# The start of a two-layer decoder trunk: GpSimd loads more of it, and its first turn stands in another order

## The chip, the cores and the metric

The kernel runs on one core of a Trainium2 chip. The metric is the device time of one execution in microseconds. Of the kernel before, three runs give a median of 1202.78 us (1201.39 to 1202.89). One more execution was recorded by the hardware profiler; all rows below come from it.

The names of the engines: PE is TensorE's matmul (PEld its weight load), DVE is VectorE, ACT is ScalarE, POOL is GpSimd, SP is SyncE, which here only issues DMAs. SP and POOL each have a DMA queue of their own (q1 and q0 in the profile), and both use the same 16 DMA engines.

## The reference

Two layers over one sequence of 512 tokens with 1024 channels, all in float32. The change lies in the first layer's first half, which is

```python
shift, scale, gate = adaln_params(c, ada_w[0, 0], ada_b[0, 0])   # silu(c) @ w + b, cut in three
hn = modulate(h, norm_g[0, 0], shift, scale)                     # rmsnorm(h, g) * (1 + scale) + shift
...
u = h @ w_in                                                     # s5_mixer: 64 groups of 16 channels
...
bu_re = jnp.einsum('blgc,gpc->blgp', u_c, bb_re)                 # each group drives 64 complex states
...
y = jnp.einsum('blgp,gcp->blgc', hs_re, cr) - jnp.einsum('blgp,gcp->blgc', hs_im, ci)
```

with a complex diagonal scan over time between the last two, then a gelu, a gated linear unit, an output product and the residual. What follows (a gated ConvFFN, an attention layer, a second ConvFFN, a final norm) is not touched.

## The kernel before

Channels lie on the 128 partitions, in eight tiles (`KT`), and time on the free axis. The start (L1189 to L1260) stands in a block whose order is written by hand for PE, ACT, DVE and SP (`manual_schedule`), the loop over the eight tiles of the state-space layer (from L1315) in a second block of that kind, which also fixes POOL. In each block an engine keeps the order of the code; a scheduler sets how the rows of both blocks follow each other on an engine.

The start, in the order of the code:

- SP loads `first` (c, the state-space parameters), x as `h` (4 transfers), `rest`, then the adaLN weights `raw<-in_ada_w`, 512 KB each. They go into three rings of buffers (`raw`, 3; `w_hi`, 5; `w_lo`, 5), so a load waits until PE has read what lay in its buffer.
- ACT squares x tile by tile, PE sums the squares over the partitions with a matrix of ones (L1197, eight products), ACT copies the sums (L1199), PE turns them (L1202).
- DVE works out the parameters of the state space from `first` (`s5_params`, small instructions of 32 to 256 columns): powers of the complex decay (`s5_pr`, `s5_pi`), the input factors (`s5_lr`, `s5_li`), the magnitude `s5_mag8`; within them the inverse root of the mean square (L427 to L437). POOL works out the turn angles (`s5_turns`).
- `ada_pe(i, (1,))` is *scale*: four steps of two weights each, four column groups of PE at a time (L226), ACT copies the result (`ada_rows`, L235), PE adds the bias and turns it (L165, L170), and DVE makes `ga` of it. DVE then forms `a_x` = h times ga times the inverse root, eight instructions (L1212).
- `ada_pe(i, (0,))` is *shift*, in the same way; between its steps PE takes the products of the first output tile, `first_tile` (L1223), which need only `a_x` and the first input matrix. Since shift is a constant along time, its part of the first tile is a column, `col` (L1245), that ACT adds on evacuation (`uf`, L1259). For the other tiles ACT adds shift to `a_x` (`shift_x`, L1252).
- B (`s5_b`) and C (`s5_rr`) are loaded by SP behind shift's weights; ACT copies B with its signs (`s5_signs_b`, L833 and L834) and flips C's (`s5_signs_c`, L839).

Then a turn for each tile m: `project` (L1270) multiplies a tile of `w_in` into u; `s5_states_in` and `s5_states_out` make tables of 1024 columns on DVE (L994, L1004); `s5_inputs` (L1032) combines them on PE, ACT evacuates them to the matrices `w1` and `kt` (L1037, L1041); `s5_kernel` stores `kt` to a table `s_z` in memory (L1050), `s5_toeplitz` reads it back shifted as `tw` (L1057), and ACT masks it (L1066). u goes to memory and back in another layout (L1276, L1280). `s5_blocks` (L1090) puts u into the states, DVE scans (L1106 to L1121), PE takes the outputs from inputs (L1131) and states (L1142), ACT applies the gelu (`yg`, L1155). Between these stand the steps of `ada` and `ada2`, which make the gate of this half and the scale and shift of the next one with the same L226.

POOL loads what the turns need. What holds it back are small additions called `gate` (L1317, L1343, L1372): each reads two numbers of a tile, so POOL's later instructions wait until that tile is there. Before, the first gate reads `mag8`, the second `tw` of turn 0, the third `tw` of turn 1. Some 23 loads of adaLN weights pass behind them.

## Time and profile before

| | |
|---|---|
| three runs, median (lowest, highest) | 1202.78 us (1201.39, 1202.89) |
| the profiled execution | 1208.49 us |
| its span, first to last instruction | 1206.7 us |
| busy: PE, PE's weight loads, DVE, ACT, POOL | 1178.1, 1019.4, 1009.1, 614.8, 122.9 us |
| granted PE clock, mean over the span | 0.994 |
| moved by DMA | 182.00 MB, of it 137.94 on SP's queue, 41.95 on POOL's |

Each row of an order of time gives start and duration in us, engine, line, operation, output and input tiles, shapes and count; rows of one kind that follow each other are merged, and brackets at the end give the idle time of the engine before the row and what ended it. A row of a stage gives its limits, its length, then for PE, PE's weight load, DVE, ACT and POOL the busy time with the count, and at the end the granted PE clock, the DMA engines' busy share and GB/s. Rows of DMA issues give the count, the size of each and the median time from issue to landing. L194 is the helper that issues every load of a `raw` tile.

### The profile page before, as it was taken

Reading aid. Unit: us, or ns where it says so; the run is one execution under the profiler, and the core shown is the slowest. Engines: PE = TensorE matmul, PEld = TensorE weight load, DVE = VectorE, ACT = ScalarE, POOL = GpSimd, SP = SyncE. Lnnn points to the kernel's source line nnn. Section 1 sums busy time; section 2 is a strip of 40 time slices with the busy share of each in tenths; the row PEclk is TensorE's granted clock in tenths of the full one; section 3 lists DMA queues with packets and bytes.
Section 4 is the critical chain, followed back from the end, with each engine's and each line's share of the span. In section 5 each row is a group of like instructions: output and inputs, shape, how many; then the busy total and the mean of one; then the engine's idle time right before and its main releaser. Section 6 shows DMA issues by size and latency. Waiting matters only on the chain.

```text
span 1206.7 us, 20655 instructions
## 1 busy us (share of the span) xinstructions
PE 1178.1 (98%) x7925; PEld 1019.4 (84%) x7925; DVE 1009.1 (84%) x1843; ACT 614.8 (51%) x1179; POOL 122.9 (10%) x228
## 2 busy tenths in 40 slices
PE   7999999999999999999999999999999999999997
PEld 2566678898989889999899888878989999999987
DVE  8888987879899999998787678876899888888865
ACT  3545554435544445555443566664466555545543
POOL 3121112100000000000000344430000000000000
PEclk9989999999999999999999999999999999999999
DMA  9598767821365454433445444433223442323331
GB/s 350 189 326 288 221 220 274 274 88 50 124 195 158 149 177 161 144 115 86 135 157 187 165 149 135 147 121 99 61 71 97 122 125 85 108 89 110 110 101 71
DMA packets 71826, 182.00 MB, mean 151 GB/s; under 512 B 23103, under 2 KB 24479, under 8 KB 70703
## 3 DMA queue, kind: packets, MB, share of 16 engines
q1 hardware_dynamic: 58767, 137.94, 35.7%
q0 software_dynamic: 11632, 41.95, 10.2%
q8 instruction: 62, 1.02, 0.3%
q10 hardware_dynamic: 1328, 0.79, 0.2%
q14 instruction: 37, 0.30, 0.1%
HBM read 173.73 MB, written 6.92 MB: 150 GB/s over the span
## 4 chain that ended last, share of the span: by engine, by line
PE 52%; DVE 21%; DMA 7%; issue 4%; ACT 2%; DVEq 0%; ACTq 0%; SPq 0%
PE mmp L317 31%; PE mmp L586 8%; DVE w_lo L301 7%; PE aux L586 3%; DMA rawd<-in_w_down 3%; DMA raw<-in_w_up 2%; DVE sums L554 2%; DVE conv L638 2%; DVE h L399 2%; DVE nm_t L554 2%; PE aux L1757 2%; PE mmp L1312 2%; PE aux L1737 2%; PE mmp L1598 2%; DVE ada_raw L270 1%
## 5 line engine op out<-in xcount | busy, mean ns | idle before, releaser
L301 DVE TENSOR_TENSOR w_lo<-raw,w_hi 128x1024 fp32r<-128x1024 f32 (+4 forms) x173 | 184.2, 1069 | 24.4 <-ACT w_hi L300 23.8
L300 ACT ACTIVATE w_hi<-raw 128x1024 fp32r<-128x1024 f32 (+4 forms) x173 | 153.9, 899 | 95.2 <-PE mmp L317 43.3
L317 PE MATMUL mmp<-ghi,w_lo 128*128 128x512 f32 (+1 forms) x412 | 147.9, 359 | 1.1 <-DVE w_lo L301 1.1
L317 PE MATMUL mmp<-ghi,w_hi 128*128 128x512 f32 (+1 forms) x412 | 148.4, 360 | 0.2 <-DVE h L399 0.2
L317 PE MATMUL mmp<-glo,w_hi 128*128 128x512 f32 (+1 forms) x412 | 147.8, 359 | 0.0
L586 PE MATMUL mmp<-w_hi 128*128 128x256 f32 x420 | 116.6, 278 | 1.8 <-ACT nm_h L593 0.7
L317 PE MATMUL mmp<-a_hi,w_hi 128*128 128x512 f32 (+1 forms) x320 | 116.6, 367 | 1.5 <-ACT a_hi L469 1.5
L586 PE MATMUL mmp<-w_lo,w_hi 128*128 128x256 f32 x420 | 116.1, 276 | 0.0
L586 PE MATMUL mmp<-w_hi,w_lo 128*128 128x256 f32 x420 | 115.9, 277 | 0.0
L317 PE MATMUL mmp<-a_hi,w_lo 128*128 128x512 f32 (+1 forms) x320 | 114.3, 358 | 0.0
L317 PE MATMUL mmp<-a_lo,w_hi 128*128 128x512 f32 (+1 forms) x320 | 114.0, 357 | 0.0
L301 DVE TENSOR_TENSOR w_lo<-sums,w_hi 128x1024 fp32r<-128x1024 f32 x78 | 94.8, 1218 | 0.0
L300 ACT ACTIVATE w_hi<-sums 128x1024 fp32r<-128x1024 f32 x78 | 81.0, 1054 | 24.5 <-DVE sums L554 22.8
L593 ACT ACTIVATE nm_h<-mmp 128x256 f32<-128x256 f32 x105 | 39.2, 380 | 103.2 <-PE mmp L586 103.1
L317 PEld LDWEIGHTS mmp<-ghi,w_lo 128*128 128x128 f32 x412 | 77.7, 189 | 13.5 <-DVE w_lo L301 1.7
L317 PEld LDWEIGHTS mmp<-ghi,w_hi 128*128 128x128 f32 x412 | 77.7, 189 | 11.0 <-issue 0.3
L317 PEld LDWEIGHTS mmp<-glo,w_hi 128*128 128x128 f32 x412 | 77.8, 189 | 10.3
L586 PEld LDWEIGHTS mmp<-w_hi 128*128 128x128 f32 x420 | 78.8, 188 | 2.7 <-ACT w_hi L300 1.4
L399 DVE SCALAR_TENSOR_TENSOR h<-mmp,par,h 128x512 f32<-128x512 f32 (+1 forms) x104 | 68.7, 663 | 14.4 <-PE mmp L317 14.3
L586 PE MATMUL mmp<-a_hi,w_lo 128*128 128x256 f32 x280 | 77.7, 278 | 1.2 <-DVE w_lo L301 1.1
L586 PEld LDWEIGHTS mmp<-w_lo,w_hi 128*128 128x128 f32 x420 | 78.9, 188 | 0.0
L586 PEld LDWEIGHTS mmp<-w_hi,w_lo 128*128 128x128 f32 x420 | 78.7, 188 | 0.1
(336 smaller groups left out, 3129.5 us busy)
## 6 DMA issues: line engine op xcount, KB each, us to landing
raw<-in_w_up SPq DMA_DIRECT2D x88, 512.0 KB, 4.0
ada_raw<-in_ada_t POOLq DMA_DIRECT2D x40, 512.0 KB, 4.1
raw<-in_ada_w POOLq DMA_DIRECT2D x24, 512.0 KB, 6.7
nf<-nfd SPq DMA_DIRECT2D x8, 1152.0 KB, 6.6
raw<-in_ada_w SPq DMA_DIRECT2D x16, 512.0 KB, 9.2
raw<-in_fox_qk SPq DMA_DIRECT2D x16, 512.0 KB, 3.5
raw<-in_w_down SPq DMA_DIRECT2D x24, 320.0 KB, 3.0
rawd<-in_w_down SPq DMA_DIRECT2D x24, 256.0 KB, 3.2
```

The source lines that it names most:

```text
L300: self.rounded = nc.scalar.activation(hi, src, AF.Copy).ins
L301: return nc.vector.tensor_tensor(lo, src, hi.bitcast(F32), ALU.subtract)
L317: self.last_mm = self.nc.tensor.matmul(o if len(xt.shape) == 2 else by_place(o), wt, xt, start=(k == 0 and n == 0), stop=(k == nk - 1 and ...
L399: add = self.nc.vector.scalar_tensor_tensor(h, ps, self.par[i][:, 16 + m:17 + m], h, op0=ALU.mult, op1=ALU.add,)
L554: sub = lambda o, u, v, op=ALU.subtract: nc.vector.tensor_tensor(o, u, v, op)
L586: self.last_mm = nc.tensor.matmul(o, wt[:, k], xt[:, k], start=(first and k == 0 and n == 0), stop=(k == H - 1 and n == 2), skip_group_che ...
L593: a = nc.scalar.activation(t, o, AF.Copy)
L638: c = nc.vector.scalar_tensor_tensor(t[:, d:], ps[:, :S - d], cw[:, 2 - d, f:f + 1], t[:, d:], op0=ALU.mult, op1=ALU.add)
L1312: nc.tensor.matmul(gps[m], wt[m][:, k], xt[:, k], start=(k == 0 and n == 0), stop=(k == KT - 1 and n == 2))
L1598: self.last_mm = nc.tensor.matmul(ps[q, b][:, :n], xt[:, k, tb], wt, start=(k == 0 and i == 0), stop=(k == KT - 1 and i == 2),)
L1737: nc.tensor.transpose(pt[:, r - rs[0], k, :], s[:, r, k * P:(k + 1) * P], self.ident)
L1757: nc.tensor.matmul(pv[:, c * P:], self.v[:, hp, k, r].rearrange("p t d -> p (t d)"), pp[:, r, c + 3 * k:NB + 3 * k, :].rearrange("p b t -> ...
```

## The change

- Eleven products of the matrix of ones with itself are put on PE ahead of the sums of squares.
- The parameters of the state space are cut at one more place, and scale's first step stands on PE directly behind the sums of squares, ahead of the turning of the sums. On DVE the largest step of the powers (`power[2]`, six instructions) moves behind `a_x`.
- SP loads the first input matrix ahead of shift's weights, not between them.
- B, the second input matrix (`load_w(1)`) and C are loaded by POOL, behind a new gate that reads shift's `ada_rows`. POOL's order in the first block is now written by hand too.
- The gate on `mag8` is gone. The gate ahead of the first adaLN loads of the turns reads u of turn 0 in place of `tw` of turn 0.
- In turn 0, `s5_states_out` stands ahead of the turn tables, B's signs behind the first `shift_x`, C's among the later ones, and the evacuation of the third projection behind `s5_inputs`. In turn 1 the last step of `ada` stands at the turn's end.

```diff
+WARM = 11
...
-        nc.sync.dma_start(b, self.io["s5_b"])
+        self.loads.dma_start(b, self.io["s5_b"])
...
         in_turn(root, power[0] + power[1])
+        yield y
         in_turn(power[2])
-        yield y
         in_turn(last)
...
+                    for _ in range(WARM):
+                        nc.tensor.matmul(ps[:, :P], ones, ones, start=True, stop=True)
...
+                    params = self.s5_params(keep, tp, self.first["s5_prm"], stats[:, :, 0])
+                    next(params)
+                    scale = self.ada_pe(i, (1,), late=True)
+                    next(scale)
                     for b in range(NB):
                         nc.tensor.transpose(stats[:, b], rows[:, b * P:(b + 1) * P], self.ident)
...
+                    load_w(0)
                     shift = self.ada_pe(i, (0,), late=True)
                     next(shift)
-                    load_w(0)
...
-                    self.s5_tables(self.rot, slice(0, G // 2), 0, 3)
-                    self.s5_consts(keep, tp)
-                    self.s5_signs_b()
-                    x_in = {0: self.s5_states_in(0)}
-                    nc.sync.dma_start(self.rr, self.io["s5_c"])
-                    load_w(1)
...
+                    self.loads = nc.gpsimd
+                    nc.gpsimd.tensor_tensor(gate, self.rows[:, 0:1], self.rows[:, 1:2], ALU.add)
+                    self.s5_consts(keep, tp)
+                    load_w(1)
+                    nc.gpsimd.dma_start(self.rr, self.io["s5_c"])
+                    self.s5_tables(self.rot, slice(0, G // 2), 0, 3)
+                    first_tile((5, 6))
...
-                gate = keep.tile([P, 1], F32, name="s5_gate")
-                nc.gpsimd.tensor_tensor(gate, self.mag8[:, 0:1], self.mag8[:, 1:2], ALU.add)
-                self.loads = nc.gpsimd
                 load_d(0)
                 load_w(2)
                 load_d(1)
                 load_w(3)
                 load_d(2)
                 read_u(0)
+                nc.gpsimd.tensor_tensor(gate, us[0][:, 0, 0:1], us[0][:, 0, 1:2], ALU.add)
+                next(ada)
+                for k in range(3, KT):
+                    shift_x(k)
+                    if k == 5:
+                        self.s5_signs_c()
+                steps, done = project(1)
+                run(steps)
+                w2s[0] = self.s5_states_out(0)
                 turns = self.s5_rotations(0)
...
-                nc.gpsimd.tensor_tensor(gate, tws[0][:, 0, 0, 0:1], tws[0][:, 0, 0, 1:2], ALU.add)
-                next(ada)
...
+                    inputs(m + 1)
+                    if not m:
                         done()
-                    inputs(m + 1)
...
                             next(ada)
                             next(ada2)
-                            next(ada)
...
+                    if m == 1:
+                        next(ada)
```

POOL, from the last of the turn angles to the first adaLN loads of the turns. `raw` from `in_s5_w_in` are input matrices (before: the third and the fourth), `dd` are tables of the skip term. Before:

```order
L1317 TENSOR_TENSOR s5_gate_533<-s5_mag8_181 128x1
L1284 DMA dd_535<-in_s5_dd 128x128
L194 DMA raw_537<-in_s5_w_in 128x1024
L1284 DMA dd_539<-in_s5_dd 128x128
L194 DMA raw_541<-in_s5_w_in 128x1024
L1284 DMA dd_543<-in_s5_dd 128x128
L1343 TENSOR_TENSOR s5_gate_533<-tw_618 128x1
L194 DMA raw_622<-in_ada_w 128x1024
```

Now (the first `dd` stands further up, among POOL's first memsets):

```order
L893 MEMSET s5_pi_316 128x32
L195 DMA raw_548<-in_s5_w_in 128x1024
L1292 DMA dd_550<-in_s5_dd 128x128
L195 DMA raw_552<-in_s5_w_in 128x1024
L1292 DMA dd_554<-in_s5_dd 128x128
L1242 TENSOR_TENSOR s5_gate_127<-ada_rows_483 128x1
L829 DMA s5_b_488<-in_s5_b 128x1024
L195 DMA raw_490<-in_s5_w_in 128x1024
L1245 DMA s5_rr_137<-in_s5_c 128x1536
L1330 TENSOR_TENSOR s5_gate_127<-u_556 128x1
L195 DMA raw_560<-in_ada_w 128x1024
```

The third and the fourth matrix (`raw_548`, `raw_552`), which stood behind a gate, stand behind none now; the new gate stands behind them, and B, the second matrix (`raw_490`) and C behind it. The adaLN loads wait for u, no longer for tw.

SP's queue at the start, from `rest` to the first store of u. Before:

```order
L126 DMA rest<-in_rest 128x408
L194 DMA raw<-in_ada_w 128x1024 x10
L194 DMA raw<-in_s_w_in 128x1024
L194 DMA raw<-in_ada_w 128x1024 x6
L828 DMA s_b<-in_s_b 128x1024
L1235 DMA s_rr<-in_s_c 128x1536
L194 DMA raw<-in_s_w_in 128x1024
L1237 DMA s_z<-s_zero 7x8x128
```

Now:

```order
L127 DMA rest<-in_rest 128x408
L195 DMA raw<-in_ada_w 128x1024 x8
L195 DMA raw<-in_s_w_in 128x1024
L195 DMA raw<-in_ada_w 128x1024 x8
L1238 DMA s_z<-s_zero 7x8x128
```

The first input matrix has moved ahead of two of shift's eight weights, and B, C and the second matrix have left the queue.

ACT in turn 1, from the evacuation of a projection to the gelu of turn 0. Before:

```order
L1275 ACTIVATE uf<-mmp 128x512
L1019 ACTIVATE s_both_138<-s_rr 64x2x64 x2
L235 ACTIVATE ada_rows<-mmp 128x512
L986 ACTIVATE rot<-rot 128x512
L1075 ACTIVATE cf<-s_mask,s_mag_181 128x2x64 x4
L980 ACTIVATE rot<-s_rot 128x16x8
L1155 ACTIVATE yg<-aux 128x256 x2
```

Now:

```order
L1283 ACTIVATE uf<-mmp 128x512
L1021 ACTIVATE s_both_139<-s_rr 64x2x64 x2
L988 ACTIVATE rot<-rot 128x512
L1077 ACTIVATE cf<-s_mask,s_mag_189 128x2x64 x4
L982 ACTIVATE rot<-s_rot 128x16x8
L236 ACTIVATE ada_rows<-mmp 128x512
L1157 ACTIVATE yg<-aux 128x256 x2
```

`ada_rows`, which waits for PE, has moved from ahead of `rot`, `cf` and `rot` to behind them.

## The prediction

> **What bounds the kernel now.** I read the page first, then the table by stage, then the start and the first turn of the state-space loop in order of time, where the change lies. On the page the first row gives busy time by engine; in the stage rows each engine has its busy time and its count, and the last three columns are the granted clock, the DMA engines' share and GB/s.

> ```profile
> PE 1178.1 (98%) x7925; PEld 1019.4 (84%) x7925; DVE 1009.1 (84%) x1843; ACT 614.8 (51%) x1179; POOL 122.9 (10%) x228
> ...
> 0.00:35.00 35.00, 27.52 (x112) 9.79 (x112) 29.52 (x146) 9.34 (x17) 12.07 (x57) 1.00 0.93 359
> ...
> 75.00:105.00 30.00, 28.79 (x240) 18.54 (x240) 24.80 (x33) 13.90 (x45) 7.45 (x15) 1.00 0.89 337
> ...
> 175.00:1207.00 1032.00, 1014.26 (x6760) 917.18 (x6758) 856.34 (x1537) 524.48 (x923) 86.63 (x124) 1.00 0.41 131
> ```

> Behind 75 us PE is busy 96 to 98% of the time: what the change does to PE's position by then reaches the end nearly whole. The first 35 us are another stage: DMA 0.93 busy, PE 27.5 of 35. What ends last there is seen in these rows of PE, its weight load, ACT and DVE (start, duration, engine, line, tile; in brackets the idle time before and its releaser).

> ```profile
> 6.28 10.32 PE L1197 MATMUL mmp<-nm_t,s_ones 128*128 128x512 f32 x16 [6.28 <-ACT nm_t L1196]
> ...
> 21.22 0.14 PEld L226 LDWEIGHTS mmp<-raw,s_sc 128*32 128x32 f32 x4 [0.63 <-DMA raw<-in_ada_w]
> ...
> 24.61 5.36 DVE L1212 SCALAR_TENSOR_TENSOR a_x<-h,ga,aux 128x512 f32<-128x512 f32 x8
> ...
> 34.21 1.05 PE L226 MATMUL mmp<-raw,s_sc 128*32 128x512 f32 x4 [0.19 <-DMA raw<-in_ada_w]
> ...
> 35.37 0.60 ACT L235 ACTIVATE ada_rows<-mmp 128x512 f32<-128x512 f32 x1 [10.58 <-PE mmp L226]
> ```

> Scale's last weight (21.2) and shift's last weight (34.2) are both waited for from DMA. From then on PE runs without a gap into the first turn:

> ```profile
> 40.69 7.11 PE L1270 MATMUL mmp<-a_x,raw 128*128 128x512 f32 x16
> ...
> 47.64 2.34 PE L1032 MATMUL aux<-s_both,x 128*128 128x160 f32 x16
> ...
> 50.87 0.32 SPq L1050 DMA_DIRECT2D s_z<-kt  x1
> ...
> 57.41 2.58 ACT L1066 ACTIVATE t<-tw,first 128x128 f32<-128x128 f32 x8 [4.21 <-DMA tw<-s_z]
> ...
> 57.96 2.34 PE L1032 MATMUL aux<-s_both,x 128*128 128x160 f32 x16
> ...
> 60.84 2.12 PE L1131 MATMUL aux<-u,t 128*128 128x64 f32 x16 [0.54 <-ACT kt L1041]
> 62.89 3.23 PE L1142 MATMUL aux<-ua,w 64*128 64x63 f32 x32
> 66.05 3.64 PE L226 MATMUL mmp<-raw,s_sc 128*32 128x512 f32 x16
> ...
> 69.62 1.42 PE L1090 MATMUL aux<-u,w 128*64 128x64 f32 x32
> ```

> The weak place is the trip of the first kernel table through memory: stored at 50.87, read back, masked on ACT from 57.41, used by PE at 60.84. PE has other products until 60.30 and waits 0.54.

> **The change part by part.** The profiled execution took 1208.49 us (span 1206.7 us, 1.8 around it); the median of the runs is 1202.78, and I add the sum to that. 0.2% of it is 2.4 us, about what a measurement of this kernel can tell from no change.

> *Products of ones, scale behind the sums of squares.* The eight sums of squares take 10.32 us; the same shape and count takes 7.11 at 40.69, so a clock that is already up saves 3.2. The eleven products of ones stand before 6.28, where PE idles. This buys nothing by itself: scale's last weight lands at 21.2 whatever PE does. If that cover were gone it would be worth up to 3.2. What scale's earlier first step does is free a buffer, so that SP can ask for shift's weights earlier. In the next rows the DMA engines fall to 127 GB/s between 19 and 21 us, and then run at 413.

> ```profile
> 19.00:21.00 2.00, 2.00 (x20) 0.49 (x12) 1.99 (x15) 0.00 (x0) 1.92 (x8) 1.00 0.60 127
> 21.00:30.00 9.00, 8.96 (x49) 4.03 (x46) 8.00 (x17) 0.77 (x2) 2.71 (x9) 1.00 1.01 413
> ```

> Nine loads of 512 KB (524,288 bytes) stand behind scale's last; at 413 GB/s each takes 1.27 us, so without the gap shift's last lands at 21.2 + 9 x 1.27 = 32.6, a gain of 1.6.

> *GpSimd's loads.* The order shows what the words don't: the third and fourth matrix and two dd tables are now issued *before* the new gate, as soon as the turn chain is done (about 24 us; before they stood behind a gate that opened at 34). They are 1.18 MB, 2.9 us at 413 GB/s, and shift's last loads are still in flight. If the two queues share the engines, shift lands at 32.6 + 2.9 = 35.5, **+1.3** against 34.2; if SP's queue goes first, -1.6. I take +1.3 (the nearest rows are the two of s_z, below, where a transfer on SP's queue that meets GpSimd's loads is late) and keep both ends. [...] No run here yet shows two long loads side by side.

> *B, second matrix, C behind the gate.* They start after shift's rows are copied (35.97 + 1.3 = 37.3). What a gate and the loads behind it take is seen at the next gate, in rows of POOL and DMA (the last number: us from issue to landing; the 4.4 is the middle of the first two of the four loads, the two of s_z are the stores of 50.87 and of 76.7):

> ```profile
> 57.52 0.19 POOL L1343 TENSOR_TENSOR s_gate<-tw 128x1 f32<-128x1 f32 x1 [20.34 <-DMA tw<-s_z]
> 58.05 2.13 POOL L194 DMA_DIRECT2D raw<-in_ada_w  x4 [0.34 <-issue]
> ...
> raw<-in_ada_w POOLq DMA_DIRECT2D x2, 512.0 KB, 4.4
> ...
> s_z<-kt SPq DMA_DIRECT2D x1, 64.0 KB, 3.0
> ...
> s_z<-kt SPq DMA_DIRECT2D x1, 64.0 KB, 5.6
> ...
> 43.94 0.37 SPq L1280 DMA_DIRECT2D u<-s_ud  x1
> ...
> u<-s_ud SPq DMA_DIRECT2D x1, 256.0 KB, 2.8
> ```

> From gate to first issue 0.53, 0.53 for each issue, about 4.0 to the first landing and 4.8 to the second's: B at 41.9, the second matrix at 43.2. PE, which had reached project(1) at 40.69, is there at 42.0: **+1.2** of waiting, where before there was none. Bounds: 0 if the loads land as the first one does, 2.4 if C is served beside them.

> *DVE.* The six power products (0.45 each) go behind the eight a_x; DVE's next deadline is x of group 0:

> ```profile
> 21.49 0.45 DVE L915 TENSOR_TENSOR s_w<-s_pi 128x128 f32<-128x128 f32 x1
> ...
> 37.46 1.23 DVE L994 TENSOR_TENSOR x<-s_lr,s_bb 128x1024 f32<-128x1024 f32 x1 [0.69 <-ACT s_bb L834]
> ```

> It becomes ready at 37.46 - 0.69 + 2.7 = 39.5, but B's two copies on ACT, once B has landed at 41.9, end near 43.6. So DVE costs nothing; x then ends near 47.3, and PE needs it behind project(1), at 42.0 + 1.2 + 7.0 = 50.2. If B were early, the 2.7 would show on DVE, still hidden. Moving the tables and w2 about is covered by the same wait.

> *The adaLN loads ahead of the table's trip.* Their gate now waits for u instead of tw. ACT holds uf back behind B's copies (43.6) and two short instructions, so u is stored near 45 and lands, by the 2.8 and a store of about 2, near 50. GpSimd issues its four loads from about 50.6 on. The table is stored at 50.87 + 1.3 + 1.2 = 53.4, into them. Uncontended the store took 3.0, and 5.6 in the turn where loads were in flight: **+2.6** (bounds 0 and 2.6). The loads are done when tw is read, so that stays at 3.5. Who waits: ACT's masking, and PE behind it.

> *ACT in the first turn.* uf of the second projection moves behind the evacuations: -0.5 on the way from masking to L1131.

> So L1131 starts at 60.84 + 1.3 + 1.2 + 2.6 - 0.5 = 65.4, and PE, done with L1032 at 60.30 + 2.5 = 62.8, idles 2.6 instead of 0.54. Now the clock. In stage rows (PE busy first, clock third from last) and in the next turn's PE rows:

> ```profile
> 60.30:63.40 3.10, 2.56 (x26) 2.45 (x26) 2.83 (x7) 3.05 (x15) 0.00 (x0) 1.00 1.01 374
> 63.40:66.80 3.40, 3.40 (x32) 2.73 (x34) 3.37 (x4) 2.17 (x4) 0.00 (x0) 0.50 0.88 330
> ...
> 81.94 2.00 PE L1142 MATMUL aux<-ua,w 64*128 64x63 f32 x32
> 83.87 1.92 PE L226 MATMUL mmp<-raw,s_sc 128*32 128x512 f32 x16
> ...
> 86.80 0.81 PE L1032 MATMUL aux<-s_both,x 128*128 128x160 f32 x4
> ```

> Three microseconds with 2.56 busy, half of it small products, were enough for the clock to drop to 0.50; L1142 and L226 then took 62.89 to 69.62 = 6.7 instead of 3.8 (81.94 to about 85.7). With more idle time before it I take the half clock again, as before: L1090 at 65.4 + 2.05 + 6.7 = 74.2, **+4.6**; at full clock 71.2, +1.6. [...]

> *ACT in the second turn.* There PE waits for ACT's yg:

> ```profile
> 85.89 0.60 ACT L235 ACTIVATE ada_rows<-mmp 128x512 f32<-128x512 f32 x1 [4.41 <-PE mmp L226]
> 86.51 0.63 ACT L986 ACTIVATE rot<-rot 128x512 f32<-128x512 f32 x1
> 87.04 1.26 ACT L1075 ACTIVATE cf<-s_mask,s_mag 128x128 f32<-128x128 f32 x4
> 88.21 0.29 ACT L980 ACTIVATE rot<-s_rot 128x128 f32<-128x128 f32 x1
> ...
> 88.82 1.90 PE L1032 MATMUL aux<-s_both,x 128*128 128x160 f32 x12 [1.21 <-ACT yg L1155]
> ```

> The three instructions between ada_rows and yg (2.2) move into the 4.41 that ACT idled: PE's 1.21 goes, **-1.2**; nothing else is late before L1270.

> Sum: +4.6 - 1.2 = +3.4, 1202.78 + 3.4 = **1206.2**. This case's own range is 1204.5 (store and matrix each half as late) to 1209.0 (the slowest of the sixteen shares of shift's last load 1.5 later, and 1.3 more at half clock).

> **The rivals.**
> - *The clock stays full.* All waits as forecast, 3.0 less: +0.4, 1203.2. [...] Against: the drop with less idle time.
> - *SP's queue goes first (faster).* GpSimd's loads yield to shift's and to the table's store: shift -1.6, second matrix +1.2, store 0, -0.5: L1131 at 59.9, PE hardly idles there. With the clock full -0.9 - 3.0 - 1.2 = -5.1, 1197.7; with the half clock of before -2.1, 1200.7. It decides from a shift landing ahead of 34.2. For it: shift's loads are all queued by about 23, before GpSimd's. Against: the 5.6 of the store.
> - *Later turns take it up.* What the first turn loses is idle time that the next turns had anyway, and the order does not do what its words say on the bound: about 1202. Against: PE 28.79 of 30 in the next turns.

> **How the numbers follow.** Forecast 0.47; full clock 0.18; SP first 0.28, half of it with the full clock; taken up later 0.07. Slower by over 0.2% (above 1205.2) is the forecast, 0.47. Faster (below 1200.4) is SP first at full clock and part of its other half, 0.20. The rest, 0.33, is within. The range leaves out the lower half of SP first at full clock and the forecast's last tail: 1198.0 to 1209.0.

> **What would show it.** Right: the last shift step on PE near 35.5, project(1) waiting about 1 us for the second matrix, the store of s_z taking over 5 us, L1131 idle by 2 to 3 us with tw as the cause further up, a clock of 0.50 behind it, no wait for yg in the second turn. Wrong: shift at 33 or earlier, or a full clock through the first turn.

## The result, and the profile after

The changed kernel takes **1213.8 us** (median of four runs, 1212.61 to 1217.02) against 1202.55 us (1201.39 to 1202.89), a ratio of 1.0099 (95% interval 1.0079 to 1.0120). It is slower, as forecast, but by 11.3 us instead of 3.4. The profiled execution took 1217.02 us (span 1215.2).

The first row of its page, and PE, SP and ACT in order of time from shift's last step to the second turn:

```profile
PE 1187.5 (98%) x7947; PEld 1026.2 (84%) x7947; DVE 1010.8 (83%) x1843; ACT 615.1 (51%) x1179; POOL 122.2 (10%) x231
```

```profile
35.18 1.05 PE L227 MATMUL mmp<-raw,s_sc 128*32 128x512 f32 x4 [0.18 <-DMA raw<-in_ada_w]
36.16 1.98 PE L1230 MATMUL mmp<-a_x,raw 128*128 128x512 f32 x4
...
38.12 1.03 PE L171 MATMUL aux<-sel,ada_rows 128*128 128x2 f32 x8
39.42 1.06 PE L1257 MATMUL aux<-par,raw 128*128 128x1 f32 x8 [0.27 <-ACT par L179]
40.34 2.06 PE L1230 MATMUL mmp<-a_x,raw 128*128 128x512 f32 x2
42.19 1.71 PE L1257 MATMUL aux<-par,raw 128*128 128x1 f32 x8
43.46 1.23 DVE L996 TENSOR_TENSOR x<-s_lr,s_bb 128x1024 f32<-128x1024 f32 x1 [5.13 <-ACT s_bb L835]
43.76 8.80 PE L1278 MATMUL mmp<-a_x,raw 128*128 128x512 f32 x16
52.40 2.34 PE L1034 MATMUL aux<-s_both,x 128*128 128x160 f32 x16
...
55.62 0.32 SPq L1052 DMA_DIRECT2D s_z<-kt  x1
...
62.71 2.34 PE L1034 MATMUL aux<-s_both,x 128*128 128x160 f32 x16
65.72 0.52 ACT L1068 ACTIVATE t<-tw,first 128x128 f32<-128x128 f32 x1 [5.46 <-DMA tw<-s_z]
...
68.67 3.68 PE L1133 MATMUL aux<-u,t 128*128 128x64 f32 x16 [3.62 <-ACT kt L1043]
72.27 3.68 PE L1144 MATMUL aux<-ua,w 64*128 64x63 f32 x32
75.88 2.89 PE L227 MATMUL mmp<-raw,s_sc 128*32 128x512 f32 x16
78.70 1.15 PE L1092 MATMUL aux<-u,w 128*64 128x64 f32 x32
...
95.62 2.44 PE L1034 MATMUL aux<-s_both,x 128*128 128x160 f32 x16
```

In the kernel before, product 7 and the column were these rows:

```profile
38.94 1.10 PE L1223 MATMUL mmp<-a_x,raw 128*128 128x512 f32 x2
39.88 0.95 PE L1245 MATMUL aux<-par,raw 128*128 128x1 f32 x8
```

Shift's last step starts 0.97 us later than before. Product 7 of the first tile takes 2.06 us (before 1.10) and project(1) 8.80 (7.11): the clock is down there (0.51). Then L1133 stands 3.62 us for the tile that ACT has just masked, and the clock is down again (0.50). In the second turn L1034 no longer waits for yg. Stages of the same kernel (PE busy first, the clock third from last) and its DMA issues (last number: us to landing):

```profile
36.90:40.30 3.40, 3.13 (x21) 2.34 (x19) 1.36 (x4) 1.11 (x4) 1.76 (x4) 1.00 0.55 180
40.30:47.20 6.90, 6.90 (x16) 3.92 (x16) 3.71 (x4) 6.39 (x11) 0.00 (x0) 0.51 0.58 216
...
67.60:77.90 10.30, 9.23 (x60) 7.57 (x64) 8.00 (x9) 6.24 (x21) 2.02 (x3) 0.50 0.39 117
```

```profile
s_z<-kt SPq DMA_DIRECT2D x1, 64.0 KB, 6.5
```

As a milestone I take one small product in the third turn, the turning of `sc`, behind which the program is unchanged; of the kernel before, then of the changed one:

```profile
98.54 0.27 PE L1388 MATMUL aux<-rest,sc 128*8 128x128 f32 x1
```

```profile
105.88 0.27 PE L1395 MATMUL aux<-rest,sc 128*8 128x128 f32 x1
```

At the milestone the change stands 7.34 us behind. From it to the end of the span the two traces take 1108.2 and 1109.3 us, and those of the experiments 1104.8 to 1110.4 (but one, below): differences of this size behind the milestone are taken here as scatter.

### The profile page after: what moved, and what is told of

It is laid out like the page before. It is cut to its first block, busy times and chain, and to the rows that moved or that the text cites. A ratio compares the mean times of both kernels' runs of the same rounds, so it can differ in the third digit from the quotient of the medians.

```text
span 1215.2 us, 20702 instructions
## 1 busy us (share of the span) xinstructions
PE 1187.5 (98%) x7947; PEld 1026.2 (84%) x7947; DVE 1010.8 (83%) x1843; ACT 615.1 (51%) x1179; POOL 122.2 (10%) x231
## 4 chain that ended last, share of the span: by engine, by line
PE 55%; issue 19%; DVE 13%; DMA 9%; ACT 2%; POOL 1%; SPq 0%; DVEq 0%; POOLq 0%; ACTq 0%
PE mmp L318 24%; PE mmp L587 12%; PE aux L587 5%; DVE w_lo L302 4%; PE mmp L1278 3%; PE mmp L1606 2%; DMA raw<-in_w_up 2%; DMA raw<-in_ada_w 2%; PE aux L1745 1%; PE aux L1034 1%; PE aux L1144 1%; DVE conv L639 1%; PE mmp L227 1%; DVE sums L555 1%; DMA ada_raw<-in_ada_t 1%
## 5 line engine op out<-in xcount | busy, mean ns | idle before, releaser
L594 ACT ACTIVATE nm_h<-mmp 128x256 f32<-128x256 f32 x105 | 39.5, 381 | 105.8 <-PE mmp L587 105.6
L587 PE MATMUL mmp<-a_hi,w_hi 128*128 128x256 f32 x280 | 78.0, 279 | 1.2 <-ACT nm_h L594 1.1
## 6 DMA issues: line engine op xcount, KB each, us to landing
raw<-in_w_up SPq DMA_DIRECT2D x88, 512.0 KB, 3.6
ada_raw<-in_ada_t POOLq DMA_DIRECT2D x40, 512.0 KB, 4.1
raw<-in_ada_w POOLq DMA_DIRECT2D x24, 512.0 KB, 6.7
raw<-in_ada_w SPq DMA_DIRECT2D x16, 512.0 KB, 9.9
raw<-in_fox_qk SPq DMA_DIRECT2D x16, 512.0 KB, 3.6
rawd<-in_w_down SPq DMA_DIRECT2D x24, 256.0 KB, 3.4
```

What stands on the lines that cost most here:

```text
L587: self.last_mm = nc.tensor.matmul(o, wt[:, k], xt[:, k], start=(first and k == 0 and n == 0), stop=(k == H - 1 and n == 2), skip_group_che ...
L594: a = nc.scalar.activation(t, o, AF.Copy)
```

## The experiments

The experiments were timed beside the kernel before, in five rounds each; 0.001 of a ratio is 1.2 us. The changed kernel was not timed again with them: its ratio comes from the four runs above, where the kernel before had a median of 1202.55 us, against 1204.3 to 1204.7 us beside the experiments. Differences to its row are the less certain for it. "Milestone" is the start of that product in the profiled execution, "shift over" the start and duration of the PE row with shift's last step added up, and the last column PE's idle time ahead of the first turn's output products (a dash: the trace shows no wait). These three columns come from one execution per kernel, and scatter too: f3_turn2 leaves the front of the kernel before as it is and has shift over 0.59 us earlier.

| kernel | ratio, 95% interval | milestone | shift over | L1133 idle |
|---|---|---|---|---|
| before | 1 | 98.54 | 35.26 | 0.54 |
| changed kernel | 1.0099 [1.0079, 1.0120] | 105.88 | 36.23 | 3.62 |
| e1_tile6 | 1.0074 [1.0052, 1.0096] | 104.81 | 36.40 | 3.84 |
| e2_tw_gate | 1.0057 [1.0035, 1.0079] | 101.87 | 36.39 | - |
| e3_both | 1.0047 [1.0031, 1.0062] | 99.59 | 37.38 | - |
| e4_no_ones | 1.0069 [1.0052, 1.0087] | 101.84 | 36.44 | 3.39 |
| f2_w23_late | 1.0023 [1.0011, 1.0035] | 99.24 | 33.33 | - |
| f1_loads_sp | 1.0002 [0.9989, 1.0014] | 94.86 | 33.50 | - |
| f3_turn2 | 0.9998 [0.9982, 1.0014] | 94.25 | 34.67 | - |
| f4_front | 0.9979 [0.9967, 0.9990] | 93.67 | 33.18 | - |
| g2_u_gate | 1.0053 [1.0036, 1.0071] | 101.84 | 35.08 | 4.18 |
| g3_w2_late | 0.9974 [0.9962, 0.9986] | 92.21 | 33.05 | - |
| g1_fill | 1.0148 [1.0115, 1.0181] | 104.75 | 36.44 | - |
| h1_fill4 | 1.0066 [1.0042, 1.0091] | 102.45 | 36.80 | - |

### Product 6 back in its place (e1_tile6)

```diff
-                    first_tile((5, 6))
+                    first_tile((5,))
                     next(shift)
+                    first_tile((6,))
```

> The changed kernel with product 6 of the first projection put back behind shift's last step, as before the change; all else as changed. Theory A (the short products): the half-clock stretch at 40.3 us stands there because the 3.4 us ahead of it hold little but products of 1, 2 and 8 columns; with a full product among them the clock stays at 1.00, the seventh product goes from 2.06 back to 1.10 us, project(1) from 8.80 to about 7.1, and the run is 2.5 to 3.5 us shorter, about 1210.5. Rival P (the phase): the steps of the clock run in a fixed beat of 3.4 us from where it came up, at 6.2 us instead of 12.2, and what stands in one window by chance decides; then the stretch stays or moves, and the time stays within 1 us of 1213.8.

```profile
42.82 7.10 PE L1279 MATMUL mmp<-a_x,raw 128*128 128x512 f32 x16 [0.86 <-DMA raw<-in_s_w_in]
...
66.26 3.67 PE L1133 MATMUL aux<-u,t 128*128 128x64 f32 x16 [3.84 <-ACT kt L1043]
```

```profile
64.70:78.40 13.70, 12.14 (x90) 8.93 (x92) 8.27 (x10) 6.73 (x23) 4.93 (x9) 0.50 0.51 141
```

The half clock at 40 us is gone: project(1) takes 7.10 again, and only now is its 0.86 us wait for the second matrix seen. But L1133 waits as long as ever for the tile, and the clock is halved from 64.7 to 78.4. The ratio falls by 0.0025, as theory A had it (2.5 to 3.5 us), though the two intervals overlap.

### The gate back on tw, alone and with the former (e2_tw_gate, e3_both)

```diff
-                nc.gpsimd.tensor_tensor(gate, us[0][:, 0, 0:1], us[0][:, 0, 1:2], ALU.add)
-                next(ada)
...
                 tws[0] = self.s5_toeplitz(0)
+                nc.gpsimd.tensor_tensor(gate, tws[0][:, 0, 0, 0:1], tws[0][:, 0, 0, 1:2], ALU.add)
+                next(ada)
```

> The changed kernel with GpSimd's gate ahead of the adaLN loads back on the Toeplitz tile tw, and these loads behind it, as before the change. Theory A (the store shares the DMA engines): the store s_z<-kt goes from 6.5 back to about 3.0 us, the products L1133 start 3.5 us earlier (about 65.2), PE's wait of 3.6 us there nearly goes, and the run is 3 to 4.5 us shorter, about 1210.0. Rival B (the store is slow for another reason, the write of ud1 beside it): the store stays above 5 us and the time within 1 us of 1213.8.

> Both edits in one: product 6 back behind shift's last step and the gate back on tw. Theory A: the two costs add, 6 to 8 us shorter, about 1207. Rival C: they hide one another (an earlier project(1) only waits longer for tw, or the half clock at 67.6 eats the gain), and it is no faster than the better of the two alone, about 1210.

DMA and PE rows of e2_tw_gate, then PE rows of e3_both:

```profile
s_z<-kt SPq DMA_DIRECT2D x1, 64.0 KB, 1.8
```

```profile
63.66 1.89 PE L1133 MATMUL aux<-u,t 128*128 128x64 f32 x16
...
75.74 0.78 PE L1034 MATMUL aux<-s_both,x 128*128 128x160 f32 x4 [2.86 <-DVE m L1109]
```

```profile
43.65 7.11 PE L1279 MATMUL mmp<-a_x,raw 128*128 128x512 f32 x16 [0.71 <-DMA raw<-in_s_w_in]
...
75.16 0.78 PE L1034 MATMUL aux<-s_both,x 128*128 128x160 f32 x4 [2.86 <-DVE m L1109]
```

The store takes 1.8 us instead of 6.5, and L1133 no longer waits: theory A of e2_tw_gate holds, and its rival B falls. Whether the two costs add (0.0025 and 0.0042 apart, 0.0052 together) the ratios can't tell, with intervals of 0.0016 to 0.0022 to either side. A wait that the late tile had covered comes out in the second turn, 2.86 us for VectorE's scan. e3_both runs at full clock up to the end of its work and is still 0.0047 slower than the kernel before: the clock is not the whole loss. Two stages of e3_both (the clock third from last):

```profile
5.70:98.00 92.30, 85.55 (x506) 45.86 (x505) 79.41 (x208) 43.17 (x117) 23.14 (x65) 1.00 0.79 294
98.00:1203.00 1105.00, 1089.01 (x7424) 968.93 (x7422) 926.05 (x1622) 568.60 (x1055) 98.00 (x145) 1.00 0.43 138
```

### Without the products of ones (e4_no_ones)

The two lines of the loop over `WARM` are taken out.

> The changed kernel without the 11 products of ones; all else as changed. Theory A: scale's last product waits for its weight, not for the clock, so the sums of squares take 10.3 us again and nothing behind them moves; within 1 us of 1213.8, the half-clock stretch at 40.3 us stays. Rival P (the phase): the clock comes up some 6 us later in another beat, the stretch at 40.3 moves or goes, and the time changes by 2 to 4 us either way.

Sums of squares and product 7 of this run, then the sums of the changed kernel:

```profile
6.25 9.01 PE L1200 MATMUL mmp<-nm_t,s_ones 128*128 128x512 f32 x16 [6.25 <-DVE s_ring L755]
...
40.55 1.11 PE L1228 MATMUL mmp<-a_x,raw 128*128 128x512 f32 x2
```

```profile
5.95 7.57 PE L1202 MATMUL mmp<-nm_t,s_ones 128*128 128x512 f32 x16
```

The sums of squares take 9.0 us instead of 7.6 and scale's first step starts 1.75 us later (15.19 against 13.44), but by shift's last step that is gone (over at 36.44 against 36.23). The half clock at 40 us, which theory A expected to stay, isn't there in this trace, though product 6 still stands where the change put it: its place alone does not make the stretch. Where the clock's steps fall (rival P) takes part in it: by the count of the last section, the step from 36.6 to 40.0 us holds 1.60 us of streamed columns here, and the step ahead of the stretch 0.91 to 1.14 in the four traces that have it with product 6 moved. The ratio is no higher than the changed kernel's, and the intervals overlap: the products buy nothing here, and whether they cost is not settled.

### The loads (f2_w23_late, f1_loads_sp)

f2_w23_late is e3_both with

```diff
+                nc.gpsimd.tensor_tensor(gate, self.rr[:, 0, 1, 0:1], self.rr[:, 0, 1, 1:2], ALU.add)
                 load_d(0)
                 load_w(2)
```

> The kernel of e3_both with the third and fourth matrix and the planes dd held behind C's landing by a second gate on GpSimd; B, C and the second matrix stay behind the first. Theory A (two requests share the DMA engines): shift's weights have them alone, its last step starts at 33 to 34 us instead of 35.7, everything behind it moves up by 1.5 to 2.5, and the run is 1 to 3 us shorter than e3_both, about 1209. Rival B (VectorE, which stands for B, sets the first turn): shift is earlier and so is B, yet the time stays within 0.7 us of e3_both, 1210.9.

f1_loads_sp is e3_both with B, C and the second matrix on SP and the gate on `mag8` back:

```diff
-                    self.loads = nc.gpsimd
-                    nc.gpsimd.tensor_tensor(gate, self.rows[:, 0:1], self.rows[:, 1:2], ALU.add)
                     self.s5_consts(keep, tp)
+                    nc.sync.dma_start(self.rr, self.io["s5_c"])
                     load_w(1)
-                    nc.gpsimd.dma_start(self.rr, self.io["s5_c"])
...
+                nc.gpsimd.tensor_tensor(gate, self.mag8[:, 0:1], self.mag8[:, 1:2], ALU.add)
+                self.loads = nc.gpsimd
                 load_d(0)
```

> The kernel of e3_both with B, C and the second matrix asked for by SyncE behind shift's weights again, and the third and fourth matrix behind the gate on the power products, as before the change; the products of ones, the early step of scale, the first matrix ahead of shift's weights and the orders of both turns stay as changed. Theory A (GpSimd's loads are what is left of the cost): shift's last step starts at 34 us or earlier (e3_both 35.7), project(1) waits for no weight and starts by 41 (43.65), VectorE does not stand 5 us for B, PE's wait of 2.9 us for the scan in the second turn goes, and the run is 7 to 10 us shorter than e3_both, 1201 to 1204, level with the kernel before or 1 to 2 us under it. Rival B (the first turn's new order on ScalarE and VectorE costs by itself): the loads give back 2 to 3 us and it stays over 1206.

Rows and a stage of f2_w23_late, then rows of f1_loads_sp:

```profile
32.17 1.16 PE L227 MATMUL mmp<-raw,s_sc 128*32 128x512 f32 x8
...
40.08 8.63 PE L1279 MATMUL mmp<-a_x,raw 128*128 128x512 f32 x16 [1.18 <-DMA raw<-in_s_w_in]
```

```profile
39.70:43.10 3.40, 3.02 (x4) 1.50 (x5) 2.75 (x3) 1.82 (x4) 0.25 (x1) 0.51 0.58 234
```

```profile
32.16 1.34 PE L227 MATMUL mmp<-raw,s_sc 128*32 128x512 f32 x8
...
38.92 7.11 PE L1277 MATMUL mmp<-a_x,raw 128*128 128x512 f32 x16
...
70.43 0.78 PE L1034 MATMUL aux<-s_both,x 128*128 128x160 f32 x4 [2.86 <-DVE m L1109]
```

With the third and fourth matrix held back, shift's last two steps run without a wait and are over at 33.33 us (e3_both 37.38): 0.0024, or 2.9 us, as A forecast. project(1) then stands 1.18 us for the second matrix, which is the prediction's 1.2. In this trace the clock halves for 3.4 us behind that wait, with product 6 back in its place (project(1) takes 8.63 us), and again at 74 (L1279 from 73.73 takes 8.73 us, in e3_both from 75.77 at full clock 7.03), so its milestone is only 0.35 us ahead of e3_both's. With the remaining loads back on SP that wait goes too, and another 0.0021 with it. Theory A fails in one point: the wait for the scan stays at 2.86, so it does not come from B's late landing but from the order of the instructions: with the order of the kernel before (f4_front, below) it is 1.00.

### Parts of the change on the kernel before (f3_turn2, f4_front)

f3_turn2 moves only the last `next(ada)` of the second turn; f4_front has that, the products of ones, scale's early step, the first matrix ahead of shift's weights and the place of `power[2]`, as in the change's diff.

> The kernel before with only the last adaLN step of the second turn behind the factors and rotations, as the change has it. Forecast: PE's wait of 1.2 us for yg goes, ratio to the kernel before 0.999 (1.2 us shorter). Rival: ScalarE's work is only moved and PE waits for the next turn's tile instead: 1.000.

> The kernel before with the change's front alone (products of ones, scale's first step ahead of the transposes, the first matrix ahead of shift's weights, the last power products behind a_x) and the second turn's order. Forecast of the prediction's terms: SyncE asks for shift's weights earlier, the last lands 1.6 us earlier (32.6 against 34.2 us), yg's wait goes: 1.5 to 3 us shorter than the kernel before, ratio 0.998. Rival: the transfers in front of shift's weights set their landing whatever SyncE asks, and only yg's 1.2 us are won.

PE of f3_turn2, then of f4_front:

```profile
63.29 2.36 PE L226 MATMUL mmp<-raw,s_sc 128*32 128x512 f32 x16
65.58 1.15 PE L1090 MATMUL aux<-u,w 128*64 128x64 f32 x32
...
83.99 2.44 PE L1032 MATMUL aux<-s_both,x 128*128 128x160 f32 x16
```

```profile
32.12 1.06 PE L227 MATMUL mmp<-raw,s_sc 128*32 128x512 f32 x8
...
69.23 0.78 PE L1034 MATMUL aux<-s_both,x 128*128 128x160 f32 x4 [1.00 <-DVE m L1109]
```

f3_turn2's L1032 runs its 16 without the wait for yg, but the time doesn't tell it from the kernel before; its 1.2 us lie inside the interval. f4_front is faster than both kernels. Its shift weights are there in time, and so they are in g3_w2_late (shift over at 33.18 and 33.05 us): the prediction's -1.6 shows. It does not in every execution, as g2_u_gate below, with the same order in front, has 35.08. Beside f1_loads_sp f4_front differs in the order of the first turn and of the first block's last instructions (tables, B's signs, POOL's order), which costs 0.0023, and the scan's wait is 1.00 instead of 2.86.

### The gate alone on the fastest (g2_u_gate), and one step further (g3_w2_late)

g2_u_gate is f4_front with the gate on u and `next(ada)` behind it. g3_w2_late is f4_front with

```diff
+                    if m == 1:
+                        w2s[1] = self.s5_states_out(1)
...
-                    w2s[m + 1] = self.s5_states_out(m + 1)
+                    if m:
+                        w2s[m + 1] = self.s5_states_out(m + 1)
```

> The kernel of f4_front, the fastest so far, with one part of the change more: GpSimd's gate for the adaLN weights on the first tile u, so that they are asked for ahead of the table's trip through DRAM. Theory A (they share the DMA engines with the trip's store): s_z<-kt takes 5 to 6.5 us instead of about 3, PE waits 2 to 4 us for the tile at L1133 and the clock halves behind it; the gain of 1 us at L227 (weights there in time) is lost in that; 2 to 5 us longer than f4_front, 1204 to 1207. Rival B: with project(1) earlier the store goes ahead of the weights and nothing is lost, within 1 us of 1202.3.

> The kernel of f4_front with VectorE's three operations for the second tile w2 moved out of the first turn, behind the second turn's scan and table. Theory A (the scan stands behind them on VectorE, and PE's L1034 waits 1.0 us for the scan): that wait goes, 0.5 to 1.5 us shorter than f4_front. Rival B: what is moved delays the states of a later turn on VectorE and PE waits there, 0 to 3 us longer.

PE, a stage and the store of g2_u_gate; PE of g3_w2_late:

```profile
64.30 3.67 PE L1133 MATMUL aux<-u,t 128*128 128x64 f32 x16 [4.18 <-ACT kt L1043]
```

```profile
63.90:74.10 10.20, 9.80 (x64) 7.57 (x64) 7.28 (x7) 5.09 (x17) 1.97 (x4) 0.50 0.50 125
```

```profile
s_z<-kt SPq DMA_DIRECT2D x1, 64.0 KB, 6.6
```

```profile
65.86 2.44 PE L1034 MATMUL aux<-s_both,x 128*128 128x160 f32 x16
```

With the gate alone the ratio rises by 0.0074 (8.9 us), more than by any other part: 4.18 us of waiting, then 10.2 us at half clock. In its profiled execution shift was also over 1.9 us later than in f4_front's; the gate stands behind that, so this part of the trace is not its doing. The expectation had the mechanism and half the size. g3_w2_late takes the last wait for the scan away; its milestone is 1.46 us earlier, its ratio no different from f4_front's within the intervals, and clearly below 1.

### Filling PE's wait (g1_fill, h1_fill4)

The changed kernel with eight, or four, idle products ahead of L1133:

```diff
+                    if not m:
+                        fill = self.mm.tile([P, S], F32, name="mmp")
+                        for _ in range(8):
+                            nc.tensor.matmul(fill, ones, x[:, 0], start=True, stop=True)
                     yp, outs = self.s5_from_inputs(us[m], t)
```

> The changed kernel with eight added products of 128x128 by 128x512, whose result nobody reads, ahead of the first turn's products L1133: PE works through the 3.6 us in which it waits for the Toeplitz tile. Theory A (the idle time is what halves the clock): the half-clock stretch of 10.2 us behind the wait is gone or one step of 3.4 us at most, L1133 to L227 take 5.9 instead of 10.2 us, and the run is 2 to 4 us shorter than the changed kernel's 1213.8. Rival P (the clock falls in its own beat whatever PE does, or for the small products): the stretch stands, time unchanged; where the added products end behind the tile, up to 1 us longer.

> The kernel of g1_fill with four added products instead of eight: in g1_fill one took 0.89 us, so four take 3.55 us and end as the Toeplitz tile lands (65.1 to 68.6 us). Theory A (PE's idle 3.6 us halve the clock behind them, and the later half-clock stretches of g1_fill belong to its 7.1 us of added work): no half clock at 67.6, the third turn's first products stand 4 us earlier than the changed kernel's (98.54 us there in the kernel before, 105.88 in the changed one, about 101.5 here), and the run is 2 to 4 us shorter than 1213.8. Rival Q (the chip allows so much work in a time, and what is added at one place is taken at another): the stretch at 67.6 goes and another comes later, and the time stays at 1213 to 1216.

Two stages of g1_fill; PE and a stage of h1_fill4:

```profile
170.40:173.80 3.40, 1.97 (x15) 1.35 (x13) 3.23 (x5) 3.40 (x11) 0.00 (x0) 1.00 0.03 12
173.80:180.60 6.80, 6.80 (x35) 5.86 (x34) 6.80 (x10) 0.69 (x2) 1.57 (x3) 0.50 0.72 207
```

```profile
65.52 3.60 PE L1405 MATMUL mmp<-a_x,s_ones 128*128 128x512 f32 x8
68.95 1.89 PE L1133 MATMUL aux<-u,t 128*128 128x64 f32 x16
```

```profile
65.50:74.60 9.10, 9.10 (x76) 5.62 (x74) 8.59 (x15) 7.96 (x26) 0.00 (x0) 1.00 0.28 99
```

With four products the clock stays at 1.00, L1133 to L227 take 5.6 us instead of 10.0 (68.95 to 74.56, against 68.67 to 78.70), the milestone stands 3.43 us earlier, and the ratio falls by 0.0033 (the intervals just overlap): theory A in the trace, where no later stretch stands that the two kernels do not have as well (421 us; 425 and 433 there). The time does not decide: the median, 1213.5 us, lies in rival Q's range as well. One of h1_fill4's six executions took 4174 us, for a reason that the record does not show; its ratio and this median are those of the other five. g1_fill's eight products were over only 3.3 us behind the tile; the half clock behind them is gone too (1.00 from 47.5 to 173.7 us), but the run is slower, against both theories. Its trace shows a new stretch of 6.8 us at half clock from 173.8, behind 3.4 us in which PE worked 1.97. There PE waits 1.43 us for ScalarE's masking, ahead of which ScalarE waits 0.99 us for a weight (`s_w_glu`) from DMA; why that weight is late, and why this kernel's runs spread from 1214.8 to 1229.4 us, stays open.

## Why the prediction was wrong in size

The direction and most of the mechanisms were right; 11.3 us came out where 3.4 were forecast.

- **Right.** Shift's last step started at 35.18 (forecast 35.5), and the two queues shared the engines: from 27 to 31 us of the changed kernel's trace SP's queue moved 0.86 MB and GpSimd's 0.80, together at 418 GB/s. f2_w23_late fits that, where the third and fourth matrix are held back and the steps are over some 4 us earlier than in e3_both (33.33 against 37.38). The -1.6 ahead of it shows in f4_front and g3_w2_late; the wait for the second matrix in f2_w23_late (1.18) and e1_tile6 (0.86), while in the changed kernel the half clock hid it. The tile came late by way of the store, and PE's wait for yg went.
- **The step that failed: "I take the half clock again, as before".** The forecast had one stretch of 6.8 us. The changed kernel has 6.9 us at 40.3, not foreseen at all, and 10.3 us at 67.6. The first makes product 7, the column and project(1) 3.4 us longer (2.06 for 1.10, 1.71 for 0.95, 8.80 for 7.11). The prediction has no term for the line that moved product 6, and that line bears on it: ahead of the stretch PE was busy for 3.13 of 3.40 us, but mostly with products of 1, 2 and 8 columns. Of the five traces with product 6 moved, four have the stretch (the changed kernel, e2_tw_gate, g1_fill, h1_fill4) and e4_no_ones has not; e1_tile6 and e3_both, with it back, have none, and f2_w23_late has one behind its wait for the second matrix. So the line takes part, but is not the only condition. The second runs from L1133 to L1092, 10.0 us where the forecast had 8.8. The store's term was too small besides: 3.5 us were added (3.0 to 6.5), not 2.6. L1092 starts at 78.70 instead of 74.2; of these 4.5 us 2.2 are there when project(1) is over (52.40 instead of 50.2), 0.9 come from the store and 1.3 from the second stretch.
- **The base.** I added the sum to the median, but made it against a profiled execution that was itself at half clock for 6.8 us. f3_turn2's trace is not, and has L1090 at 65.58, where the profile before had it at 69.62: with the clock up the kernel before stands 3 to 4 us earlier, and so the loss is larger by as much. That is enough for the difference between the 7.3 us at the milestone and the 11.3 of the runs, but it is argued from one trace: no execution of the kernel before at its median was profiled, and the changed kernel's profiled execution lies 3.2 us above its own median. The store's 3.0 us, too, belonged to that execution; f3_turn2, with the same order there, has 1.5.
- **"DVE costs nothing".** No wait for it shows in the changed kernel, whose late tile hides it, but it is not free: with the tile in time the changed order shows as 2.86 us of waiting for the scan (e2_tw_gate, e3_both, f1_loads_sp).

The experiments can be put in a row, in ratios: the front and second turn -0.0021 (f4_front against 1), the first turn's order +0.0023 (to f1_loads_sp), B, second matrix and C late +0.0021 (to f2_w23_late), third and fourth matrix early +0.0024 (to e3_both), product 6 and the gate +0.0052 (to the changed kernel); together 0.0099. The kernels' intervals reach 0.0011 to 0.0022 to either side, so a step of 0.002 is only just told apart, and the last step leads to a ratio that was measured at another time.

Of the rivals, "SP's queue goes first" fell with the 35.18, "the clock stays full" with the two stretches, "later turns take it up" with the 7.34 us at the milestone. Not tried: the products of ones alone on the kernel before, and the changed kernel timed beside the experiments.

## What to carry to other kernels

Before a load is moved to a second queue, look at which small transfer with a reader waiting will be in flight beside it: here 64 KB went from 3.0 us (1.5 to 2.0 in the experiments with the adaLN loads behind it) to 6.5, and one gate was the largest part of the loss. In the four traces where PE waited 3.4 to 4.2 us for the tile, the wait was paid twice, once waiting and once at half clock behind it (10.3 us at 0.50 in the changed kernel); and a stretch of small products may cost the same without any wait, as at 40 us in the changed kernel (6.9 us at 0.51). When a forecast is made on one profiled execution, hold its mean clock (0.994 here) against those of the runs (0.996 to 0.999 in most of the runs of the kernel before), and name which half-clock stretches are its own.
